# Cached keys and values in rows of four keys per partition, with the order restored on the way, and two more steps ahead of the sample gate product

## The chip, the cores and the metric

The program runs on one core of one Trainium2 chip. A core has five engines that run side by side, each with its own instruction stream: PE (the matrix engine; its weight loads are listed apart as PEld), DVE (vector), ACT (activation functions and copies), POOL (a second elementwise engine) and SP, which here issues the transfers (DMA) between the chip's large memory and the on-chip memories: SBUF, 128 partitions wide, and PSUM, into which PE writes. The metric is device time in microseconds. The kernel before took 1937.82 us, the median of three runs.

## The reference

One inference step of a one-layer streaming encoder, in float32. There are 1024 new frames of one stream (the prompt) and 16 new frames of each of 8 running streams (the samples), whose past is 1024 cached rows each. The layer runs three token mixers on the same normalised input: a stick-breaking attention ("sb"), a state-space scan (SSD) and a forgetting attention ("fox"). Then follow an output projection, cross-attention and a feed-forward block. What the change touches is the attention of the samples over their cached rows, 4 heads of 64 in each of the two groups:

```python
def sb_attend(q, k, v, q_pos, k_pos):
    z = jnp.einsum('bqhd,bkhd->bhqk', q, k).astype(jnp.float32) * (HEAD_DIM ** -0.5)
    valid = k_pos[None, :] < q_pos[:, None]
    log_keep = jnp.where(valid, jax.nn.log_sigmoid(-z), 0.0)
    after = lax.cumsum(log_keep, axis=3, reverse=True) - log_keep
    w = jnp.where(valid, jnp.exp(jax.nn.log_sigmoid(z) + after), 0.0)
    return jnp.einsum('bhqk,bkhd->bqhd', w, v.astype(jnp.float32)).astype(q.dtype)

def fox_attend(q, k, v, fq, fk, q_pos, k_pos):
    s = jnp.einsum('bqhd,bkhd->bhqk', q, k).astype(jnp.float32) * (HEAD_DIM ** -0.5)
    s = s + (jnp.transpose(fq, (0, 2, 1))[..., :, None] - jnp.transpose(fk, (0, 2, 1))[..., None, :])
    valid = k_pos[None, :] <= q_pos[:, None]
    p = jax.nn.softmax(jnp.where(valid, s, -jnp.inf), axis=-1)
    return jnp.einsum('bhqk,bkhd->bqhd', p, v.astype(jnp.float32)).astype(q.dtype)
...
        sb_k = jnp.concatenate([past['sb_k'].astype(sk.dtype), sk], axis=1)
...
        fcum = jnp.cumsum(jnp.concatenate([past['fox_logf'].astype(jnp.float32), logf], axis=1), axis=1)
        fox_o = fox_attend(fq, fox_k, fox_v, fcum[:, past_len:], fcum, qpos, kpos)
```

The weights of sb need a running product over the keys in their order, and those of fox the running sum `fcum` of the gates, also in the order of the keys.

## The kernel before

**Stages.** The input projections come first (to about 100 us of the span in part, and on beside attention). From about 100 to 760 us runs the attention stage: prompt units and sample units of sb and then of fox, in one list that `pipeline` steps through. A unit is `rows` (scores and weights of up to 128 queries) and, one or two units later, `av` (weights transposed, times values). After each step of the pipeline one step of a generator called the fill is taken, or 1.1 steps once the fill has come to the SSD. The fill holds what remains of the input projections (`dense`, three matmuls for each float32 product: L314, L315, L316), the gate sums `fox_sums` between them, and then the SSD. Each `yield` in the fill ends such a step. What is left of the fill after the attention stage is woven into the output projection, which follows, then cross-attention and feed-forward. A planner built into the framework then sets the order of the instructions on each engine: it has a cost for each instruction, takes the order of the code as the first priority, and gives the lines marked `high_priority` more of it. So a step that is written later moves instructions on all engines, and not only its own.

**A sample unit.** Four units p per group, each of two streams b2 of 16 queries and 4 heads. Its 1024 cached keys come in two halves. `load_k` brings half a stream's keys (512 keys x 256 numbers, 512 KB) from `cache_sb_k` or `cache_fox_k` into a buffer "wr" (L850): partition p gets keys p, 128 + p, 256 + p and 384 + p. Eight transposes (L856) turn them, four into each PSUM tile "pst", and ACT copies each tile, 128 x 512, to "kf" (L857), where a column is a key in its order. Four matmuls side by side (`quads`, L844) make the scores "pss". `sb_rows` then takes two sigmoids on ACT (L504, L505), a product scan against the order of the keys on DVE (L507), and a product on POOL (L132). In `av` the weights are transposed in blocks of 128 keys (L887), ACT copies them (L888), and the products with the values (L896) take 128 keys at a time. The values come by L905 into the buffers "vr", again with keys p, 128 + p and so on in partition p. There are 16 loads of each of the four caches, 64 in all, 64 key copies (L857), and 72 weight transposes, 8 of the nine of each unit for cached keys and one for the new ones. The buffers "wr" (two) also take the weights of the projections (L306), and "vr" and "kf" use the buffers "wh" and "wl" of their splits.

**Prompt rows.** A block of 128 queries against up to 512 keys is a product in two matmuls (L547, L548), and a third (L550) adds the mask in the last block. The scores stand in a "pss" bank until L504 and L505 have read it.

**The gate sums.** `fox_sums` makes running sums of the log gates: for the samples a scan on DVE (L687) into a tile of 32 rows, of which L688 writes each row sixteen times to the scratch `fssc`. L690 reads four pieces of it back. L692 and the product L696 make the sample gate tile `fnew`, which the fox units use. Behind the generator's next `yield` stand transposes for the convolution (L756) and the projections z (L769 stores them).

Of the kernel before, what the change touches and what calls it, by code (L numbers as in the profile page):

```python
# [17 lines left out]
P = 128  # L18
# [44 lines left out]
def tile_hybrid_step(ctx: ExitStack, tc: tile.TileContext, a: dict):  # L63
    nc = tc.nc
    ACT, DVE, POOL, PE, SP = nc.scalar, nc.vector, nc.gpsimd, nc.tensor, nc.sync
# [32 lines left out]
    def xc_t(dt=F32):  # L98
        return xcp.tile([P, 1056], dt, tag="xc", name="xc")

    def sg_t(dt=F32):
        return sgp.tile([P, 512], dt, tag="sg", name="sg")
# [7 lines left out]
    def pd():  # L110
        return ps_t(psd, "d")
# [4 lines left out]
    def pT():  # L116
        return ps_t(pst, "t")
# [34 lines left out]
    ident = cst.tile([P, P], F32, name="ident")  # L152
# [143 lines left out]
    def raw_t():  # L296
        return ring.tile([P, 1056], F32, tag="wr", name="wr", bufs=2)
# [301 lines left out]
    def sg2_t(dt=F32):  # L599
        return ptp.tile([P, 256], dt, tag="so", name="so", bufs=4)  # L600
# [45 lines left out]
    def fox_sums():  # L646
        l = log1p_exp_negabs(lf, [P, NBLK, 4])
        DVE.scalar_tensor_tensor(lf.rearrange("p a b -> p (a b)"), lf.rearrange("p a b -> p (a b)"), 0.0,
                                 l.rearrange("p a b -> p (a b)"), ALU.min, ALU.subtract)
        SP.dma_start(out=a["p_fox_logf"][0, 0].rearrange("(k p) h -> p k h", p=P), in_=lf[:, 0:8, :])  # L650
        SP.dma_start(out=a["s_fox_logf"][0].rearrange("b q h -> (b q) h"), in_=lf[:, 8, :])

        fr = xc_t()
        for hf in range(2):
            tp = pd()
            for b in range(4):
                PE.transpose(tp[:4, b * P:(b + 1) * P], lf[:, 4 * hf + b, :], ident)
            ACT.copy(fr[0:4, hf * 512:(hf + 1) * 512], tp[:4])
        DVE.tensor_tensor_scan(fr[0:4, :SEQ], fr[0:4, :SEQ], fr[0:4, :SEQ], 0.0, ALU.add, ALU.bypass)
        SP.dma_start(out=fc_sc, in_=fr[0:4, :SEQ])  # L660
        tp = pd()
        for b in range(8):
            PE.transpose(tp[:, b * 4:(b + 1) * 4], fr[0:4, b * P:(b + 1) * P], ident[:4, :4])
        DVE.tensor_copy(fqc, tp[:, :32].rearrange("p (b h) -> p b h", h=4))
        yield


        pl0 = sg_t()[:, :256]
        SP.dma_start(out=pl0.rearrange("p (u h) -> p u h", h=4),
                     in_=a["cache_fox_logf"][0].rearrange("b k h -> (b k) h").rearrange("(u p) h -> p u h", p=P))  # L670
        pl1 = sg_t()[:, :256]
        DVE.tensor_copy(pl1.rearrange("p (k b h) -> p k b h", k=8, h=4),
                        pl0.rearrange("p (b k h) -> p k b h", k=8, h=4))
        sr = xc_t()[0:32, :PAST + DEC_S]
        for hf in range(2):
            tp = pd()
            for b in range(4):
                PE.transpose(tp[:32, b * P:(b + 1) * P], pl1[:, (4 * hf + b) * 32:(4 * hf + b + 1) * 32], ident)
            ACT.copy(sr[:, hf * 512:(hf + 1) * 512], tp[:32])
        x8 = sg2_t()  # L680
        DVE.tensor_tensor(out=x8[:, :32].rearrange("p (b h) -> p b h", h=4),
                          in0=lf[:, 8, :].unsqueeze(1).to_broadcast([P, 8, 4]),
                          in1=smask.unsqueeze(2).to_broadcast([P, 8, 4]), op=ALU.mult)
        tp = pd()
        PE.matmul(tp[:32, :16], x8[:, :32], fold, start=True, stop=True)
        ACT.copy(sr[:, PAST:], tp[:32, :16])
        DVE.tensor_tensor_scan(sr, sr, sr, 0.0, ALU.add, ALU.bypass)  # L687
        SP.dma_start(out=fs_sc, in_=sr.unsqueeze(1).to_broadcast([32, DEC_S, PAST + DEC_S]))  # L688
        for p in range(4):
            SP.dma_start(out=fqs[:, p:p + 1], in_=fs_sc[8 * p:8 * p + 8, 0, PAST:PAST + DEC_S])  # L690
        y8 = sg2_t()
        DVE.tensor_tensor(out=y8[0:32, :P].rearrange("p (b t) -> p b t", t=DEC_S),  # L692
                          in0=sr[:, PAST:].unsqueeze(1).to_broadcast([32, 8, DEC_S]),
                          in1=bmask32.unsqueeze(2).to_broadcast([32, 8, DEC_S]), op=ALU.mult)
        tp = pd()
        PE.matmul(tp[:, :P], hsel, y8[0:32, :P], start=True, stop=True)  # L696
        DVE.tensor_copy(fnew, tp[:, :P])
        yield
# [112 lines left out]
    def decode_units(m):  # L811
# [15 lines left out]
        def rows(p):  # L827
# [19 lines left out]
            def load_k(hf, b2):  # L847
                raw = raw_t()
                rv = raw[:, :1024].rearrange("p (k c) -> p k c", c=256)
                SP.dma_start(out=rv, in_=ck[2 * p + b2, hf * 512:(hf + 1) * 512, :]  # L850
                             .rearrange("(k p) c -> p k c", p=P))
                kf = ring.tile([P, 1056], F32, tag=("wh", "wl")[b2], name="kf")
                for nb in range(2):
                    tp = pT()
                    for k in range(4):
                        PE.transpose(tp[:, k * P:(k + 1) * P], rv[:, k, nb * P:(nb + 1) * P], ident)  # L856
                    ACT.copy(kf[:, nb * 512:(nb + 1) * 512], tp)  # L857
                return kf

            def emit_past(hf):  # L860
                def emit(ps):
                    kf = [load_k(hf, b2) for b2 in range(2)]
                    quads(ps, lambda b2, nb: kf[b2][:, nb * 512:(nb + 1) * 512])
                return emit
# [13 lines left out]
        def av(p, w, hold):  # L878
# [4 lines left out]
            for k0 in (0, 4, 8):  # L883
                nk = min(4, 9 - k0)
                tp = pT()
                for k in range(nk):
                    PE.transpose(tp[:, k * P:(k + 1) * P], w[:, (k0 + k) * P:(k0 + k + 1) * P], ident)  # L887
                ACT.copy(wn if k0 == 8 else wt[:, k0 * P:(k0 + 4) * P], tp[:, :nk * P])  # L888

            po = pO()  # L890
# [10 lines left out]
            for hf in range(2):  # L901
                raws = []
                for b2 in range(2):
                    raw = ring.tile([P, 1056], F32, tag=("wh", "wl")[b2], name="vr")
                    SP.dma_start(out=raw[:, :1024].rearrange("p (k c) -> p k c", c=256),  # L905
                                 in_=cv[2 * p + b2, hf * 512:(hf + 1) * 512, :]
                                 .rearrange("(k p) c -> p k c", p=P))
                    raws.append(raw)
                for k in range(4):
                    work += quads(wt[:, (4 * hf + k) * P:(4 * hf + k + 1) * P],  # L910
                                  lambda b2, nb, raws=raws, k=k: raws[b2][:, k * 256 + nb * P:k * 256 + (nb + 1) * P],
                                  False, hf == 1 and k == 3)
# [644 lines left out]
    q = []  # L1557
    drain(x_query(0, q))
    for hd in range(1, 4):
        att = both(hd - 1, q)  # L1560
        q = []
# [375 lines left out]
```

## Time and profile before

| what | value |
|---|---|
| median of three runs | 1937.82 us (1937.67 to 1940.25) |
| profiled execution | 1935.64 us, span 1933.8 us |
| mean granted clock of PE | 0.983 |
| PE busy | 1843.4 us, 95% of the span |
| DVE, ACT, POOL busy | 46%, 42%, 32% |
| moved by DMA | 307.52 MB, 159 GB/s on average |
| stage 100 to 760 us: PE, DVE, ACT, POOL busy | 601.44, 328.02, 327.37, 266.72 us |

The profile is of one execution, and its rows are in microseconds of its span. A row of the timeline gives the start, the length, the engine, the line of the code and the operation with the tile that is written, an arrow and the tiles that are read. In brackets stands how long the engine had been idle and which instruction or transfer ended that. A row of a window gives the busy time of PE, PEld, DVE, ACT and POOL in that stretch with the number of instructions, the clock that PE was granted (1.00 is full speed), the busy share of the DMA engines and the rate in GB/s.

### The profile page before, as it was taken

The numbers are of one execution on the slowest core, as the hardware profiler recorded it, in microseconds if no ns is written. First come the engines' busy times: TensorE is split into PE (matmuls) and PEld (weight loads), VectorE is DVE, ScalarE is ACT, GpSimd is POOL, SyncE is SP. The second block draws the span as 40 slices with busy tenths as digits, with TensorE's granted clock in tenths as the row PEclk, the third lists the DMA queues.
The fourth block names the chain that finished last, engine by engine and source line by source line (L and its number), as shares of the span: only waits on it lengthen the run. The fifth ranks groups of instructions, "written<-read, shape, count | busy, mean of one in ns | idle before, by whom it ended". The sixth has DMA issues, their size and how long they took to land.

```text
span 1933.8 us, 32139 instructions
## 1 busy us (share of the span) xinstructions
PE 1843.4 (95%) x12128; PEld 1646.3 (85%) x12128; DVE 898.4 (46%) x1802; ACT 816.6 (42%) x1702; POOL 628.4 (32%) x918
## 2 busy tenths in 40 slices
PE   7989997999898899999999999999999999999997
PEld 5889776898876677889998888999999999888886
DVE  3421324466646783354445378333333333455554
ACT  6431543444656772143333165333333333344443
POOL 6632415263424563211101213554544443000000
PEclk9999997999999989999999999999999999999999
DMA  9455646455487878435559123322233223557572
GB/s 335 139 163 152 205 124 171 131 147 163 139 256 244 259 236 299 153 124 164 164 166 342 59 95 97 95 69 69 72 78 89 71 69 90 193 195 237 176 241 90
DMA packets 328923, 307.52 MB, mean 159 GB/s; under 512 B 88637, under 2 KB 292517, under 8 KB 328769
## 3 DMA queue, kind: packets, MB, share of 16 engines
q1 hardware_dynamic: 328768, 305.48, 51.5%
q8 instruction: 95, 1.56, 0.3%
q14 instruction: 60, 0.48, 0.1%
HBM read 229.31 MB, written 76.11 MB: 158 GB/s over the span
## 4 chain that ended last, share of the span: by engine, by line
PE 79%; DMA 6%; DVE 4%; ACT 2%; POOL 1%; issue 1%; SPq 0%; ACTq 0%; POOLq 0%; DVEq 0%
PE psd L1804 11%; PE psd L314 9%; PE psd L316 9%; PE psd L315 9%; PE pst L1804 8%; PE pss L1804 4%; PE pss L314 3%; PE pss L315 3%; PE pss L316 3%; PE pso L1804 2%; PE pso L580 2%; PE pst L314 1%; PE pst L315 1%; PE pst L316 1%; PE pst L565 1%
## 5 line engine op out<-in xcount | busy, mean ns | idle before, releaser
L132 POOL TENSOR_TENSOR wl<-wr,wh 128x256 fp32r<-128x256 f32 (+1 forms) x180 | 134.2, 778 | 241.2 <-ACT wh L289 208.9
L314 PE MATMUL psd<-act,wh 128*128 128x384 f32 x576 | 198.5, 345 | 5.2 <-DVE sg L441 2.6
L316 PE MATMUL psd<-act,wl 128*128 128x384 f32 x576 | 197.5, 343 | 0.1
L315 PE MATMUL psd<-act,wh 128*128 128x384 f32 x576 | 197.2, 342 | 0.0
L1804 PE MATMUL pst<-bT,tr 128*128 128x256 f32 (+1 forms) x1068 | 155.0, 293 | 0.0
L1804 PEld LDWEIGHTS pst<-bT,tr 128*128 128x128 f32 x1068 | 144.9, 188 | 0.1
L314 PE MATMUL psd<-wh,act 128*128 128x256 f32 (+3 forms) x414 | 134.2, 327 | 3.9 <-DMA act<-osc 1.1
L316 PE MATMUL psd<-wh,act 128*128 128x512 f32 (+3 forms) x424 | 136.9, 324 | 0.0
L315 PE MATMUL psd<-wl,act 128*128 128x256 f32 (+3 forms) x414 | 133.6, 324 | 0.5 <-POOL wl L132 0.5
L1804 PE MATMUL psd<-bT,tr 128*128 128x320 f32 (+1 forms) x912 | 133.2, 295 | 1.0 <-DVE tr L1651 0.5
L251 POOL TENSOR_SCALAR sm<-sm 128x1 f32<-128x1 f32 (+2 forms) x30 | 9.2, 307 | 377.6 <-ACT y L1899 291.8
L1804 PEld LDWEIGHTS psd<-bT,tr 128*128 128x128 f32 x912 | 124.7, 188 | 1.9 <-DVE tr L1651 0.7
L314 PEld LDWEIGHTS psd<-act,wh 128*128 128x128 f32 x576 | 109.3, 190 | 9.3 <-DVE sg L441 3.4
L132 POOL TENSOR_TENSOR tr<-u,tr 128x256 fp32r<-128x256 f32 x110 | 82.9, 782 | 99.2 <-ACT tr L1647 81.7
L132 POOL TENSOR_TENSOR ws<-ws 128x256 f32<-128x256 f32 (+2 forms) x100 | 78.5, 813 | 112.2 <-DVE ws L507 84.5
L316 PEld LDWEIGHTS psd<-act,wl 128*128 128x128 f32 x576 | 109.1, 189 | 2.0 <-issue 1.3
L315 PEld LDWEIGHTS psd<-act,wh 128*128 128x128 f32 x576 | 109.3, 190 | 0.8 <-issue 0.6
L1779 DVE TENSOR_TENSOR tr<-tr,pst 128x256 f32<-128x256 f32 (+1 forms) x86 | 38.6, 449 | 137.5 <-ACT tr L1776 104.4
L132 POOL TENSOR_TENSOR tr<-raw,tr 128x256 fp32r<-128x256 f32 x94 | 69.4, 768 | 86.2 <-ACT tr L1647 77.8
L289 ACT CAST wh<-wr 128x1024 fp32r<-128x1024 f32 (+2 forms) x45 | 47.0, 1050 | 106.2 <-PE psd L316 42.6
L314 PEld LDWEIGHTS psd<-wh,act 128*128 128x128 f32 x414 | 79.5, 192 | 11.9 <-issue 1.7
L1647 ACT CAST tr<-tr 128x384 fp32r<-128x384 f32 (+1 forms) x70 | 37.7, 538 | 122.0 <-DMA tr<-hidsc 112.8
(597 smaller groups left out, 4709.1 us busy)
## 6 DMA issues: line engine op xcount, KB each, us to landing
u<-w_down SPq DMA_DIRECT2D x40, 512.0 KB
raw<-w_down SPq DMA_DIRECT2D x26, 512.0 KB
st<-qksc SPq DMA_DIRECT2D x48, 256.0 KB
wr<-w_in SPq DMA_DIRECT2D x22, 512.0 KB
tr<-hidsc SPq DMA_DIRECT2D x57, 192.0 KB
hidsc<-tr SPq DMA_DIRECT2D x34, 288.0 KB
qksc<-sg SPq DMA_DIRECT2D x48, 192.0 KB
wr<-cache_sb_k SPq DMA_DIRECT2D x16, 512.0 KB
```

The source lines that it names most:

```text
L132: POOL.tensor_tensor(out=out[:, a0:a1], in0=in0[:, a0:a1], in1=in1[:, a0:a1], op=op)
L251: POOL.tensor_scalar(v, ss, inv, EPS, ALU.mult, ALU.add)
L289: ACT.copy(hi[:, :n], raw[:, :n])
L314: PE.matmul(out, ah, bh, start=start, stop=False)
L315: PE.matmul(out, ah, bl, start=False, stop=False)
L316: PE.matmul(out, al, bh, start=False, stop=stop)
L565: PE.transpose(tp[:, o:o + P], w[:, (2 * kp + j) * P:(2 * kp + j + 1) * P], ident)
L580: return PE.matmul(po[r:r + 64, q_], vt[:, 2 * (k0 + i) + j, :], pfs[i][:, sl], start=start and k0 == 0 and (j == 0 or qp > 0), stop=k0 + ...
L1647: ACT.copy(hi, src)
L1779: DVE.tensor_tensor(out=at(out, g), in0=at(x, g), in1=ps[g][:, :GW[g]], op=op)
L1804: PE.matmul(dst[g][:, :GW[g]], x[:, ka], y[:, k, :], start=start and k == 0 and m == 0, stop=stop and k == 3 and m == 2, skip_group_check= ...
```

## The change

The cached keys and values are loaded with four consecutive keys to a partition: partition p of a half gets keys 4p to 4p + 3, which lie side by side in memory, 4 KB in one run, where four runs of 1 KB stood before. Tile k of the four then holds keys k, 4 + k, 8 + k and so on. For the keys, the copy out of PSUM puts the order back: it reads the 512 columns with a step of 128 (k fastest) and writes them side by side. For the values, the weights are brought to the same order: each transpose of cached keys' weights reads every fourth column as its 128. The transposes, copies and products are as many and as large as before. Apart from that, two `yield`s more stand in `fox_sums` between the reads of `fssc` and the product for `fnew`.

```diff
--- before.py
+++ after.py
@@ -688,6 +688,8 @@
         SP.dma_start(out=fs_sc, in_=sr.unsqueeze(1).to_broadcast([32, DEC_S, PAST + DEC_S]))
         for p in range(4):
             SP.dma_start(out=fqs[:, p:p + 1], in_=fs_sc[8 * p:8 * p + 8, 0, PAST:PAST + DEC_S])
+        yield
+        yield
         y8 = sg2_t()
         DVE.tensor_tensor(out=y8[0:32, :P].rearrange("p (b t) -> p b t", t=DEC_S),
                           in0=sr[:, PAST:].unsqueeze(1).to_broadcast([32, 8, DEC_S]),
@@ -847,14 +849,16 @@
             def load_k(hf, b2):
                 raw = raw_t()
                 rv = raw[:, :1024].rearrange("p (k c) -> p k c", c=256)
+
                 SP.dma_start(out=rv, in_=ck[2 * p + b2, hf * 512:(hf + 1) * 512, :]
-                             .rearrange("(k p) c -> p k c", p=P))
+                             .rearrange("(p k) c -> p k c", k=4))
                 kf = ring.tile([P, 1056], F32, tag=("wh", "wl")[b2], name="kf")
                 for nb in range(2):
                     tp = pT()
                     for k in range(4):
                         PE.transpose(tp[:, k * P:(k + 1) * P], rv[:, k, nb * P:(nb + 1) * P], ident)
-                    ACT.copy(kf[:, nb * 512:(nb + 1) * 512], tp)
+                    ACT.copy(kf[:, nb * 512:(nb + 1) * 512].rearrange("c (p k) -> c p k", k=4),
+                             tp.rearrange("c (k p) -> c p k", k=4))
                 return kf
 
             def emit_past(hf):
@@ -884,7 +888,9 @@
                 nk = min(4, 9 - k0)
                 tp = pT()
                 for k in range(nk):
-                    PE.transpose(tp[:, k * P:(k + 1) * P], w[:, (k0 + k) * P:(k0 + k + 1) * P], ident)
+                    wk = w[:, 8 * P:9 * P] if k0 == 8 else \
+                        w[:, k0 * P:(k0 + 4) * P].rearrange("q (p k) -> q p k", k=4)[:, :, k]
+                    PE.transpose(tp[:, k * P:(k + 1) * P], wk, ident)
                 ACT.copy(wn if k0 == 8 else wt[:, k0 * P:(k0 + 4) * P], tp[:, :nk * P])
 
             po = pO()
@@ -904,7 +910,7 @@
                     raw = ring.tile([P, 1056], F32, tag=("wh", "wl")[b2], name="vr")
                     SP.dma_start(out=raw[:, :1024].rearrange("p (k c) -> p k c", c=256),
                                  in_=cv[2 * p + b2, hf * 512:(hf + 1) * 512, :]
-                                 .rearrange("(k p) c -> p k c", p=P))
+                                 .rearrange("(p k) c -> p k c", k=4))
                     raws.append(raw)
                 for k in range(4):
                     work += quads(wt[:, (4 * hf + k) * P:(4 * hf + k + 1) * P],
```

Lines after the two `yield`s are two higher in the changed kernel (L698 for L696, L758 for L756, L771 for L769), and further down three to six higher (L859 for L856, L902 for L896, L911 for L905, L853 for L850). Three places of the changed order follow; all are in the attention stage.

The first place is the sample gate product. On PE, before, it stands behind three prompt rows ("psd<-so,hsel" is the product, "psd<-ident,xc" the transposes behind it):

```order
L547 MATMUL pss<-st 128x128
L548 MATMUL pss<-st 128x128
L550 MATMUL pss<-mask_sb,identr 128x128
L547 MATMUL pss<-st 128x256
L548 MATMUL pss<-st 128x256
L550 MATMUL pss<-mask_sb,identr 128x128
L547 MATMUL pss<-st 128x384
L548 MATMUL pss<-st 128x384
L550 MATMUL pss<-mask_sb,identr 128x128
L696 MATMUL psd<-so,hsel 128x128
L756 MATMUL psd<-ident,xc 128x24 x8
L314 MATMUL psd<-wh,act 128x264
```

After, a piece of 512 keys from a fourth row has come in ahead of it:

```order
L547 MATMUL pss<-st 128x256
L548 MATMUL pss<-st 128x256
L550 MATMUL pss<-mask_sb,identr 128x128
L547 MATMUL pss<-st 128x384
L548 MATMUL pss<-st 128x384
L550 MATMUL pss<-mask_sb,identr 128x128
L547 MATMUL pss<-st 128x512
L548 MATMUL pss<-st 128x512
L550 MATMUL pss<-mask_sb,identr 128x128
L698 MATMUL psd<-so,hsel 128x128
L758 MATMUL psd<-ident,xc 128x24 x8
L314 MATMUL psd<-wh,act 128x264
```

That piece of L547, L548 and L550 stood 48 dense matmuls behind the product before. On POOL, before, the splits of a weight tile (wl) stand ahead of the last piece of a prompt row (ws, 127 wide):

```order
L132 TENSOR_TENSOR ws<-ws 128x256 x3
L132 TENSOR_TENSOR wl<-wr,wh 128x256 x4
L132 TENSOR_TENSOR wl<-wr,wh 128x32
L132 TENSOR_TENSOR ws<-ws 128x127
L834 MEMSET st 128x128
```

After, they stand behind it:

```order
L132 TENSOR_TENSOR ws<-ws 128x256 x3
L132 TENSOR_TENSOR ws<-ws 128x127
L132 TENSOR_TENSOR wl<-wr,wh 128x256 x4
L132 TENSOR_TENSOR wl<-wr,wh 128x32
L836 MEMSET st 128x128
```

The last piece of the row has moved ahead of five pieces of the splits.

The second place is SP at the same time, with the scratch of the gate sums (fssc, fqs) and the value loads of the sample unit. Before:

```order
L688 DMA fssc<-xc 512x1x1040
L850 DMA wr<-cache_sb_k 128x4x256
L596 DMA mixsc<-sg 64x2x256
L690 DMA fqs<-fssc 128x1x1 x4
L769 DMA zsc<-sg 128x256 x3
L905 DMA vr<-cache_sb_v 128x4x256 x2
```

After:

```order
L596 DMA mixsc<-sg 64x2x256
L688 DMA fssc<-xc 512x1x1040
L853 DMA wr<-cache_sb_k 128x1024
L690 DMA fqs<-fssc 128x1x1 x4
L771 DMA zsc<-sg 128x256
L911 DMA vr<-cache_sb_v 128x1024 x2
```

One store of z, not three, stands between the reads of fssc and the pair of value loads now, and the store to mixsc comes first. On PE that sample unit's products with the values (pso<-vr,st), before, stand behind 48 dense matmuls, two row pieces of 512 keys, 48 more dense matmuls and the row's end:

```order
L316 MATMUL psd<-wh,act 128x264
L547 MATMUL pss<-st 128x128
L548 MATMUL pss<-st 128x128
L550 MATMUL pss<-mask_sb,identr 128x128
L896 MATMUL pso<-pt,so 32x128 x4
L896 MATMUL pso<-vr,st 32x128 x16
L314 MATMUL psd<-wh,act 128x264
L315 MATMUL psd<-wl,act 128x264
L316 MATMUL psd<-wh,act 128x264
```

After, the first sixteen stand behind the first 48 dense matmuls and one product of a row:

```order
L315 MATMUL psd<-wl,act 128x264
L316 MATMUL psd<-wh,act 128x264
L547 MATMUL pss<-st 128x512
L902 MATMUL pso<-pt,so 32x128 x4
L902 MATMUL pso<-vr,st 32x128 x16
L314 MATMUL psd<-wh,act 128x264
L315 MATMUL psd<-wl,act 128x264
L316 MATMUL psd<-wh,act 128x264
```

The other sixteen come after 24 more dense matmuls, as before, and now also after the four remaining matmuls of the row.

The third place is a half's fourth key load of a later sample unit, on PE. Before, its transposes (the five of them ahead of "pst<-ident,ws") come right behind the scores of the first half:

```order
L315 MATMUL psd<-act,wh 128x384
L316 MATMUL psd<-act,wl 128x384
L856 MATMUL pst<-ident,wr 128x128 x15
L844 MATMUL pss<-kf,st 32x512 x4
L856 MATMUL pst<-ident,wr 128x128 x5
L565 MATMUL pst<-ident,ws 128x128 x4
L856 MATMUL pst<-ident,wr 128x128 x3
L565 MATMUL pst<-ident,ws 128x128 x7
L314 MATMUL psd<-act,wh 128x384
```

After, eight dense matmuls stand between:

```order
L859 MATMUL pst<-ident,wr 128x128 x8
L846 MATMUL pss<-kf,st 32x512 x4
L314 MATMUL psd<-act,wh 128x384
L315 MATMUL psd<-act,wh 128x384
L316 MATMUL psd<-act,wl 128x384
L314 MATMUL psd<-act,wh 128x384
L315 MATMUL psd<-act,wh 128x384
L316 MATMUL psd<-act,wl 128x384
L314 MATMUL psd<-act,wh 128x384
L315 MATMUL psd<-act,wh 128x384
L859 MATMUL pst<-ident,wr 128x128 x4
```

The transposes of that load now begin with four, eight matmuls later.

## The prediction

> **What bounds the kernel now.** I read the page first, for the engine that is short, and then the busy time by stretches.
>
> ```profile
> span 1933.8 us, 32139 instructions
> PE 1843.4 (95%) x12128; PEld 1646.3 (85%) x12128; DVE 898.4 (46%) x1802; ACT 816.6 (42%) x1702; POOL 628.4 (32%) x918
> ```
>
> The matrix engine PE is busy for 95% of the span; no other engine reaches half, weight loads apart. A part of the change is worth only what it takes from PE's idle time or from the time PE runs at a low granted clock. The stretches (start:end, length, then PE, PEld, DVE, ACT, POOL busy with counts, granted clock, DMA share, GB/s) say where that can be.
>
> ```profile
> 100.00:760.00 660.00, 601.44 (x4433) 518.53 (x4432) 328.02 (x730) 327.37 (x716) 266.72 (x400) 0.96 0.65 194
> 303.50:311.50 8.00, 1.59 (x11) 1.46 (x10) 7.53 (x9) 0.78 (x3) 8.00 (x8) 0.50 0.67 161
> 311.50:317.20 5.70, 5.67 (x26) 5.67 (x27) 1.21 (x2) 1.25 (x3) 5.58 (x13) 0.50 0.98 199
> 321.00:326.80 5.80, 5.80 (x49) 5.76 (x48) 1.89 (x5) 1.90 (x5) 1.23 (x2) 1.00 0.27 79
> 600.00:700.00 100.00, 84.67 (x699) 65.83 (x695) 78.39 (x213) 73.37 (x164) 58.76 (x97) 0.95 0.87 264
> 760.00:800.00 40.00, 40.00 (x177) 32.55 (x176) 9.63 (x14) 5.83 (x6) 11.29 (x16) 1.00 0.45 143
> ```
>
> The attention stage, 100 to 760, holds everything the change touches, and 660.00 − 601.44 = 58.6 us of PE idle. The second and third rows are the sample gate: 8 us with 1.59 busy, and then 5.70 us in which 26 dense matmuls run at clock 0.50, where 5.80 us at 1.00 hold 49. The stall thus costs some 6.3 us of waiting and about 2.8 of slow clock. The last row, the output projection, has no gap. PE's waits from 160 to 760 (total, times, longest) name the parties.
>
> ```profile
> PE psd L696 <- DVE so L692: 6.3, 1, 6.3
> PE pst L856 <- DMA wr<-cache_sb_k: 5.5, 4, 1.8
> PE pst L856 <- DMA wr<-cache_fox_k: 4.7, 4, 1.5
> PE pso L896 <- DMA vr<-cache_sb_v: 3.5, 2, 2.0
> PE pss L844 <- ACT kf L857: 1.2, 1, 1.2
> PE pst L856 <- ACT kf L857: 0.9, 2, 0.7
> ```
>
> The gate product is the longest, 6.3 us. Of 64 cache loads ten are waited for, 5.5 + 4.7 + 3.5 = 13.7 us in all; the other 54 land in time, so their rows are worth nothing. The copies that will be strided cost PE 2.1 us now.
>
> **The loads' rows: −1.5.** Each load moves the same 512 KB, in 4 KB runs instead of four of 1 KB. A cached-key load in the chain of waits, its transposes, and the DMA rate from 203.4 in steps of 0.1 us; then the issue of a feed-forward weight, which has 4 KB runs already, and the rate from 1703.4:
>
> ```profile
> 203.45 3.64 DMA wr<-cache_sb_k
> GB/s 0 0 0 0 0 0 0 0 0 0 0 82 164 174 51 10 123 195 307 379 379 410 369 379 399 379 399 369 384 287 220 230 230 225 174 154 154 143 143 102
> 1703.46 0.33 SPq L1879 DMA_DIRECT2D raw<-w_down  x1
> GB/s 0 0 0 0 0 0 0 0 0 0 328 82 328 205 164 246 410 369 287 492 328 492 410 343 364 364 317 272 415 384 261 215 123 16 0 0 0 0 0 0
> ```
>
> The 1 KB runs already move 370 to 410 GB/s once going, and the 4 KB ones average about the same: no gain per byte. The 4 KB load's data start 0.94 us after its issue against 1.05 and it has no slow tail at the end, though its neighbours differ. I take 0.15 us for each of the ten waits, −1.5. The bounds are 0, and −7 were half of the 13.7 to go.
>
> **The strided reads: 0.** Sixty-four copies out of PSUM and 64 weight transposes change their pattern, not their count or size.
>
> ```profile
> L857 ACT COPY kf<-pst x64: 567/588/655, 184.2 to 722.2; 128x512 f32<-128x512 f32 x64
> L888 ACT COPY st<-pst x8: 587/592/617, 225.2 to 485.0; 128x512 f32<-128x512 f32 x8
> L888 ACT COPY so<-pst x4: 245/268/273, 225.0 to 491.8; 128x128 f32<-128x128 f32 x4
> L887 PEld LDWEIGHTS pst<-ident,ws x72: 137/140/226, 222.1 to 733.7; 128*128 128x128 f32 x72
> L672 DVE COPY sg<-sg 128x256 f32<-128x256 f32 x1 | 0.3, 294 | 4.2 <-DMA sg<-cache_fox_logf 4.2
> 283.29 0.86 PEld L856 LDWEIGHTS pst<-ident,wr 128*128 128x128 f32 x8 [1.68 <-PE pss L844]
> ```
>
> From 128 to 512 elements a copy goes from 268 to 592 ns: (592 − 268)/384 = 0.84 ns an element. The trace has no read with every element apart; the nearest, L672, takes runs of four from strided places and needs 294 ns for 256 elements, as little as plain work, so I take no extra. Were an element twice as dear, a copy would take 588 + 0.84 × 512 = 1018 ns, and 64 of them 27.5 us more on ACT, most of it in ACT's own idle time (327 of 660 us busy). The upper bound is worked out with the rival below: +10. For weights, eight transposes take 0.86 us, 0.11 each, and overlap their loads; doubling 64 loads of 140 ns adds at most 9 us, and 0 if hidden. I take 0 for both; a gain is excluded, as no element is saved.
>
> **The gate product: −0.7.** It waits for DVE's L692, and this depends on POOL and DVE, not on how much PE has to do. Timelines of DVE, POOL and ACT (start, length), then PE:
>
> ```profile
> 302.02 2.66 DVE L507 TENSOR_TENSOR_SCAN ws<-ws 128x1024 f32<-128x1024 f32 x1 [3.29 <-POOL xc L712]
> 304.60 2.68 DVE L687 TENSOR_TENSOR_SCAN xc<-xc 32x1040 f32<-32x1040 f32 x1
> 307.21 1.85 DVE L507 TENSOR_TENSOR_SCAN ws<-ws 128x128 f32<-128x128 f32 x2
> 308.99 0.73 DVE L692 TENSOR_TENSOR so<-xc,bmask 32x128 f32<-32x128 f32 x1
> 307.68 3.70 POOL L132 TENSOR_TENSOR wl<-wr,wh 128x256 fp32r<-128x256 f32 x5
> 311.35 0.41 POOL L132 TENSOR_TENSOR ws<-ws 128x127 f32<-128x127 f32 x1
> 311.79 0.38 ACT L505 ACTIVATE ws<-pss 128x256 f32<-128x256 f32 x1 [1.29 <-POOL ws L132]
> 309.77 0.79 PE L696 MATMUL psd<-so,hsel 32*128 32x128 f32 x2 [6.27 <-DVE so L692]
> 320.00 0.40 PE L547 MATMUL pss<-st 128*128 128x512 f32 x1
> 320.52 0.45 PE L547 MATMUL pss<-st 128*128 128x512 f32 x1
> ```
>
> DVE's four rows run back to back from 302.02 to 309.72 in the old order and in the new one. What the two steps put ahead of the product, by the order shown with the change, is one prompt row of three matmuls: 320.52 − 320.00 = 0.52 us warm, near 1 us at half clock. It needs a score bank that ACT's L505 empties, now at 311.79 and held by POOL's 311.35 row. POOL now takes that row ahead of the 3.70 us of splits, so the bank comes at about 307.7 + 0.41 + 0.38 = 308.5, the row runs from 308.5 to 309.5 inside the wait, and the product still starts near 309.8. Gained: the row's 0.52 us later on and a little clock, −0.7, bounds −1.5 and 0. The rest of the 6.27 stays. Queued behind the product on PE are the 26 slow matmuls above, as before.
>
> **The sample values: +3.** SP's timeline, the landing in the chain of waits, and the two PE rows concerned:
>
> ```profile
> 319.88 2.54 SPq L690 DMA_DIRECT2D fqs<-fssc  x4
> 322.52 3.20 SPq L769 DMA_DIRECT2D zsc<-sg  x3
> 329.06 4.55 DMA vr<-cache_sb_v
> 327.31 1.30 PE pso L896 x40
> 333.66 1.42 PE L896 MATMUL pso<-vr,st 128*32 128x128 f32 x32 [1.97 <-DMA vr<-cache_sb_v]
> ```
>
> SP stands at the reads of fssc until the write of it has landed (319.88; 512 x 1040 elements of 4 bytes, 2.1 MB by the order's row), issues them until 322.42, and only then zsc and the second pair of value loads. In the old order PE gets to the first values at 327.3 and waits 1.97 us for the second pair. In the new one the first values stand behind the first 48 dense matmuls, not behind 96 and two prompt rows. From 311.3: 26 slow matmuls (5.7 us), 22 at 5.80/49 = 0.12 (2.6), one product of a row (0.2), 20 value products (20 × 1.30/40 = 0.65), 24 dense (2.9) and the rest of the row (0.5) bring PE to the second pair at about 324. SP, freed at 322.42, has one zsc (3.20/3 = 1.07) ahead of the pair: issued at 323.5 and 324.0, landed at 324.0 + 4.55 = 328.5. PE waits 4.5, not 1.97: +2.5, and 0.5 for slow clock behind it; +3. Bounds: 0 if the loads land sooner, +5 with 1.7 us (a third of 5) of slow clock after the stall.
>
> **The order of the key waits: −3.** With the steps moved, the planner deals the transposes out otherwise. At 375.06 below PE took up a fourth load right behind the scores of the half before; now eight dense matmuls stand between, at the stage's 601.44/4433 = 0.14 us each some 1.1 us of the 1.70.
>
> ```profile
> 375.06 0.74 PE L856 MATMUL pst<-ident,wr 128*128 128x128 f32 x5 [1.70 <-DMA wr<-cache_sb_k]
> ```
>
> Going through the sixteen places in the new order, I count five or six waits instead of eight, of about the same length: 10.2 × 5.5/8 = 7.0, −3. Bounds −6 and +3: which of these waits survive is the least sure part of the sum.
>
> **The tail: −1.** Two fill steps that stood beside attention (600 to 700: PE 84.7 of 100) end beside the output projection (40.00 of 40.00). Their matmuls leave gaps behind that other work fills only in part; bounds −1.6 and 0.
>
> **Sum.** −1.5 + 0 − 0.7 + 3 − 3 − 1 = −3.2. The profiled execution took 1935.64 us, so 1932.4; the median of the runs, 1937.82, lies 2.18 above it, so **1934.6 us**, with 1929 to 1939 as this forecast's own range. Its runs spread from 1937.67 to 1940.25; less than 0.2%, 3.9 us, can't be told from no change.
>
> **Rivals.**
>
> *The strided reads cost.* Each element of the copy's input lies 512 bytes from the one before, each weight 16 bytes. If ACT pays one more element time per element, a copy takes 1018 ns. For: no row shows such a read at full pace. Against: L672. It decides where PE already waits for copies (1.2 + 0.9 us): a half of the keys needs four copies, and the scores wait for the last. I count six halves as tight, each 4 × 0.43 = 1.7 later: +10, and with the sum's −3.2 + 0.5 for slow clock it is 1937.8 + 7.3 = **1945**. It decides from a copy of about 0.75 us on.
> The Trainium skill, "SBUF — State Buffer", section "Door 1: The DMA port swizzle (why `[64,N]` ≈ `[32,N]`)", speaks against the change here: lines of 16 bytes need two hits each, PSUM's lines are 8 bytes, and "any non-contiguous PSUM access pattern significantly slows down matmuls". It gives no price for a copy, and no run so far shows one.
>
> *The loads land before they are waited for.* If larger rows shorten a load by a microsecond, 0.7 of the 13.7 us of waits go (−9.6), with −0.7 and −1 as above and +1.5 left of the values: 1937.8 − 9.8 = **1928**. For: the longest waits are 1.8, 1.5 and 2.0 us, so that one microsecond would end most of them. Against: the equal GB/s.
>
> *The gate wait goes.* If the moved steps fill it, 6.3 us and 2.8 of slow clock fall away: 1937.8 − 9.1 = **1928.7**. Against: only one row is put there, and DVE's 302.02 to 309.72 is unmoved.
>
> **How the numbers follow.** Forecast 0.52, strided reads 0.25, loads 0.17, gate 0.06. Faster, the same and slower (by 0.2%): from the forecast 0.19, 0.29, 0.04; strided reads 0, 0.04, 0.21; loads 0.14, 0.03, 0; gate 0.05, 0.01, 0. Together 0.38, 0.37, 0.25. The range takes in both other sides, 1926 to 1946.
>
> **What would show it.** Copies at 0.57 to 0.66 us and weight loads at 0.14 confirm the zero, copies near 1.0 the first rival. The gate product should still wait for DVE, 5 us or more, and start at 309 to 311. The second pair of the sample's first values should be waited for 4 to 6 us. The eight waits of key transposes should total 6 to 8 us; under 3 speaks for the loads. I am wrong if PE's idle time from 100 to 760 changes by more than 6 us either way.

## The result and the profile after

The changed kernel took 1925.93 us, the median of six runs (1918.90 to 1928.80), beside 1940.38 us of the kernel before (1937.67 to 1941.10) on the same chip: a ratio of 0.9924 with a 95% interval of 0.9905 to 0.9943. Two later sets of runs gave 0.9937 (0.9912 to 0.9962) and 0.9934 (0.9915 to 0.9954). It is faster by some 0.6 to 0.8%, 11 to 15 us between the medians. The forecast was 1934.6 us and no clear difference; the range ended at 1926, just above the result.

The profiled execution took 1928.8 us, the slowest of its six, and that of the kernel before, 1935.64, was faster than all six of its runs. The two profiles thus show 7 us of the 14.5. The page of the changed kernel:

```profile
span 1926.9 us, 32135 instructions
PE 1842.8 (96%) x12128; PEld 1644.7 (85%) x12128; DVE 899.4 (47%) x1802; ACT 816.7 (42%) x1702; POOL 627.6 (33%) x918
q1 hardware_dynamic: 304192, 305.48, 51.1%
```

PE has the same work, 1842.8 against 1843.4 us; what fell is the time between. The row of the queue counts packets: 24,576 fewer than in the row of the kernel before, for the same 305.48 MB.

```profile
q1 hardware_dynamic: 328768, 305.48, 51.5%
```

To see where time went I took three stretches of the attention stage, and for each the loss: the time in which PE is idle, and the length times what is missing from the clock (which is rounded to a hundredth, so that the product is good to 1.3 us in 260). Idle time at a low clock enters both terms. Before, then after (columns as in the prediction):

```profile
295.00:345.00 50.00, 39.72 (x320) 36.40 (x321) 18.89 (x28) 16.81 (x39) 28.16 (x42) 0.80 0.66 164
345.00:500.00 155.00, 149.55 (x1073) 133.99 (x1071) 93.13 (x158) 77.63 (x169) 69.09 (x93) 1.00 0.52 147
500.00:760.00 260.00, 233.42 (x1762) 185.66 (x1762) 165.29 (x461) 157.58 (x345) 110.54 (x180) 0.94 0.80 250
```

```profile
295.00:345.00 50.00, 38.17 (x287) 33.52 (x287) 20.08 (x26) 17.94 (x40) 31.61 (x42) 0.76 0.63 160
345.00:500.00 155.00, 148.00 (x1058) 131.99 (x1055) 91.11 (x146) 75.07 (x165) 61.99 (x88) 0.99 0.50 145
500.00:760.00 260.00, 240.79 (x1850) 192.25 (x1849) 171.42 (x478) 160.15 (x351) 115.09 (x185) 0.99 0.80 257
```

At the sample gate (295 to 345) the loss went from 10.3 + 0.20 × 50 = 20.3 us to 11.8 + 0.24 × 50 = 23.8, so this place got worse. From 345 to 500 it rose from 5.5 to some 8.6. From 500 on it fell from 26.6 + 0.06 × 260 = 42.2 to 19.2 + 0.01 × 260 = 21.8, by 20 us, of which 7.4 are idle time and 13 are the clock. Where the missing clock is counted in the trace only while PE is busy, the gate goes from 17 to 22 us and the stretch from 500 on from 41 to 23, so the reading stands. Two more profiles of the changed kernel give 22.9 and 21.9 at the gate, 23.7 and 22.8 from 500 on. In the profiles all the gain lies where the fox units run beside the SSD, 180 us and more behind the added steps. Of PE's waits from 160 to 760, those at the gate, for cache loads and for key copies, after:

```profile
PE pss L547 <- ACT ws L505: 4.6, 1, 4.6
PE pso L902 <- DMA vr<-cache_sb_v: 3.8, 1, 3.8
PE pst L859 <- DMA wr<-cache_sb_k: 2.9, 3, 1.5
PE pst L859 <- DMA wr<-cache_fox_k: 2.2, 1, 2.2
PE pss L846 <- ACT kf L860: 1.2, 1, 1.2
PE pst L859 <- ACT kf L860: 1.0, 2, 0.8
```

The waits for cache loads fell from 13.7 us to 2.9 + 2.2 + 3.8 = 8.9, and the strided copies are waited for as long as the plain ones were (1.2 and 1.0). The 6.3 us of the gate product have only moved, to the row piece ahead of it:

```profile
306.74 0.22 PE L550 MATMUL pss<-mask_sb,identr 128*128 128x128 f32 x1
311.57 0.79 PE L547 MATMUL pss<-st 128*128 128x512 f32 x1 [4.60 <-ACT ws L505]
313.17 0.79 PE L698 MATMUL psd<-so,hsel 32*128 32x128 f32 x2 [0.27 <-DVE so L694]
```

### The profile page after: what moved, and what is told of

Its sections match the earlier page's. It is cut to its first block, busy times and chain, and to the rows that moved or that the text cites. A ratio compares the mean times of both kernels' runs of the same rounds, so it can differ in the third digit from the quotient of the medians.

```text
span 1926.9 us, 32135 instructions
## 1 busy us (share of the span) xinstructions
PE 1842.8 (96%) x12128; PEld 1644.7 (85%) x12128; DVE 899.4 (47%) x1802; ACT 816.7 (42%) x1702; POOL 627.6 (33%) x918
## 3 DMA queue, kind: packets, MB, share of 16 engines
q1 hardware_dynamic: 304192, 305.48, 51.1%
## 4 chain that ended last, share of the span: by engine, by line
PE 72%; issue 6%; DMA 6%; DVE 5%; ACT 3%; POOL 2%; SPq 0%; ACTq 0%; POOLq 0%; DVEq 0%
PE psd L1810 11%; PE pst L1810 8%; PE psd L314 8%; PE psd L315 8%; PE psd L316 8%; PE pss L1810 4%; PE pss L314 2%; PE pss L315 2%; PE pss L316 2%; PE pso L1810 2%; DMA act<-acsc 1%; PE pso L580 1%; POOL wl L132 1%; PE pst L314 1%; PE pst L316 1%
## 5 line engine op out<-in xcount | busy, mean ns | idle before, releaser
L132 POOL TENSOR_TENSOR wl<-wr,wh 128x256 fp32r<-128x256 f32 (+1 forms) x180 | 138.2, 800 | 224.7 <-ACT wh L289 188.1
L1810 PE MATMUL psd<-bT,tr 128*128 128x256 f32 (+1 forms) x912 | 132.6, 295 | 0.5 <-DVE tr L1657 0.5
L314 PEld LDWEIGHTS psd<-act,wh 128*128 128x128 f32 x576 | 109.4, 190 | 13.7 <-DVE so L735 5.0
L132 POOL TENSOR_TENSOR ws<-ws 128x256 f32<-128x256 f32 (+2 forms) x100 | 72.8, 756 | 138.2 <-DVE ws L507 113.9
L314 PEld LDWEIGHTS psd<-wh,act 128*128 128x128 f32 x414 | 79.6, 193 | 10.2 <-issue 1.3
```

The source lines that it names most:

```text
L132: POOL.tensor_tensor(out=out[:, a0:a1], in0=in0[:, a0:a1], in1=in1[:, a0:a1], op=op)
L314: PE.matmul(out, ah, bh, start=start, stop=False)
L1810: PE.matmul(dst[g][:, :GW[g]], x[:, ka], y[:, k, :], start=start and k == 0 and m == 0, stop=stop and k == 3 and m == 2, skip_group_check= ...
```

## The experiments

Two theories stood against each other, that the 4 KB rows made the gain, and that the order did in which the planner dealt the work out anew. They can be told apart: where only the pattern of a load is changed, the order of the instructions on every engine stays row for row the same.

**The rows, in four orders.** The first pair puts 1 KB rows into the changed kernel, at both loads:

```diff
-                             .rearrange("(p k) c -> p k c", k=4))
+                             .rearrange("(k p) c -> p k c", p=P))
```

> The changed kernel with the 64 cache loads put back to four runs of 1 KB a partition; strided copies, strided weights and both steps stay, and the order of the instructions on every engine is the changed kernel's own, row for row. (What it leaves out: keys and values are then in another order than the weights, so the attention of the samples is not the reference's.) If the 4 KB rows made the gain (theory of rows): the time goes back up, by 8 to 14 us against the changed kernel, to 1934 to 1940. If the new order made it (theory of order): 1925 to 1929, within 3 us of the changed kernel. By the sum of the prediction, rows were worth 1.5 us.

The second puts 4 KB rows into the kernel before, by the opposite edit.

> The kernel before with nothing changed but the 64 cache loads, now one run of 4 KB a partition; order of all instructions as before, row for row. (The order of keys is not restored, so the attention of the samples is not the reference's.) Theory of rows: 1926 to 1932, most of the gain, and waits of the key transposes and values for DMA falling from 13.7 us to under 5. Theory of order: 1937 to 1940, no difference beyond 0.2%, waits for DMA above 10 us.

The third pair is the layout without the added steps (e3) and the same with 1 KB rows (e9). Against the changed kernel, e3 is this:

```diff
-        yield
-        yield
         y8 = sg2_t()
```

> The changed loads, copies and transposes without the two added steps. Theory of rows: 1926 to 1932. Theory of order, with the gain from the two steps: 1936 to 1940. The strided copies should stay at 0.59 us and strided weight loads at 0.21 us in either case.

> The layout's copies and weights strided, but the loads as before, in 1 KB runs, and no added steps; the order of all instructions is that of the layout alone (1932.4), row for row. (The order of the keys is then wrong, so the attention of the samples is not the reference's.) Third pair for the rows: in the old order they gave -6.1 us, in the changed kernel's -2.3. If the gain of rows is steady at 2 to 6 us: 1934 to 1939. If strided reads cost: above 1940, with the loads' gain then larger.

The fourth is the added steps alone (e5) and the same with 4 KB rows, without strided reads (e10). Against the changed kernel, e10 is:

```diff
-                    ACT.copy(kf[:, nb * 512:(nb + 1) * 512].rearrange("c (p k) -> c p k", k=4),
-                             tp.rearrange("c (k p) -> c p k", k=4))
+                    ACT.copy(kf[:, nb * 512:(nb + 1) * 512], tp)
...
-                        w[:, k0 * P:(k0 + 4) * P].rearrange("q (p k) -> q p k", k=4)[:, :, k]
+                        w[:, (k0 + k) * P:(k0 + k + 1) * P]
```

> The kernel before with the two added steps and nothing else: loads of 1 KB runs, plain copies and weights. If the steps' new order makes most of what is left after the rows (rows alone gave -6.1 us of -12.6), this runs 1929 to 1934. If the order of the changed kernel was lucky because layout and steps were planned together, 1936 to 1941. The gate product waits for DVE or for a score bank, 5 us or more, in either case.

> The changed kernel with plain copies and plain weights: 4 KB loads and two steps, order of the steps alone (1933.6). (The order of the keys is then wrong, so the attention of the samples is not the reference's.) Fourth pair for the rows: 1928 to 1932 if they give 2 to 6 us in this order too; 1933 to 1935 if nothing.

The changed kernel ran again beside the first three.

> The changed kernel once more, beside the others on the same chip: 1919 to 1929 us with a median near 1926, for a second profile of it. In its profile the stage from 500 to 760 us should again hold some 15 to 19 us less idle time and slow clock than before, if that is where the gain lies; the sample gate and the values behind it should again be no better than before.

Medians, and ratios to the kernel before in the same set of runs:

| order of | with 1 KB rows | with 4 KB rows | rows |
|---|---|---|---|
| the kernel before | 1 | 1933.65: 0.9968 (0.9952 to 0.9983) | −0.32% |
| the layout alone | 1939.38: 0.9989 (0.9969 to 1.0009) | 1932.41: 0.9971 (0.9953 to 0.9989) | −0.18% |
| the steps alone | 1933.62: 0.9975 (0.9958 to 0.9992) | 1930.48: 0.9959 (0.9940 to 0.9977) | −0.16% |
| the changed kernel | 1929.39: 0.9943 (0.9927 to 0.9959) | 1927.14: 0.9937 (0.9912 to 0.9962) | −0.06% |

The rows gain in all four, on average (0.32 + 0.18 + 0.16 + 0.06)/4 = 0.18%, 3.5 us. Only the first pair is clear of its interval by itself; taken as independent, the four intervals give 0.05 to 0.31% for the average. Neither theory holds alone: with 1 KB rows the changed order still saves 0.57%, and without steps the rows and strided reads save 0.29%. Of the order's 0.57%, the steps alone give 0.25%, clear of their interval, and the layout's order alone 0.11%, not clear of it; the layout has an order of its own even without steps, on PE from 222 us on. So the strided reads are not isolated by any pair: 0.9971 with them and 0.9968 without are two orders. Neither order with them is slower than its counterpart without, beyond the intervals.

PE's waits for cache loads, in the four orders, went from 13.7 to 11.9 us with 4 KB rows, from 10.8 to 8.3, from 10.9 to 11.6 and from 12.3 to 8.9. In the kernel before they stayed far above the 5 us that the theory of rows expected, although its median fell by 6 us; where the rest of that gain arises the profiles don't show. What a 4 KB row saves in the queue can be read from the page. In the order before and in the changed one, the row of the queue, 4 KB and 1 KB (e2, then e1; the other two are above):

```profile
q1 hardware_dynamic: 304192, 305.48, 51.0%
```

```profile
q1 hardware_dynamic: 328768, 305.48, 51.8%
```

Before: 0.515 × 1933.8 = 995.9 us on each of 16 engines with 1 KB rows, 0.510 × 1934.5 = 986.6 with 4 KB; changed order: 0.518 × 1929.3 = 999.4 and 0.511 × 1926.9 = 984.6. The other two pairs differ by 13 and 9 us. So 9 to 15 us of each engine for 24,576 packets, (9.3 to 14.8) × 16/24,576 = 6 to 10 ns for each packet saved.

Where the order gains shows in the losses of the same eight kernels (1 KB rows, then 4 KB), each from one profile:

| order of | 295 to 345, us | 500 to 760, us |
|---|---|---|
| the kernel before | 20.3, 20.5 | 42.2, 41.7 |
| the layout alone | 18.1, 16.2 | 40.3, 34.4 |
| the steps alone | 24.4, 21.7 | 29.2, 30.3 |
| the changed kernel | 26.5, 23.8 | 26.6, 21.8 |

With the steps the gate is worse and the stretch from 500 on better, in either layout and with either row. The steps alone:

```profile
295.00:345.00 50.00, 37.63 (x288) 32.85 (x288) 20.05 (x26) 18.23 (x40) 30.71 (x42) 0.76 0.74 169
500.00:760.00 260.00, 238.58 (x1823) 190.28 (x1822) 169.91 (x476) 160.46 (x351) 115.35 (x187) 0.97 0.81 254
```

**The steps.** If the two steps had to stand ahead of the product, or if each step gave a fixed gain, these would show it. First both behind the product:

```diff
-        yield
-        yield
         y8 = sg2_t()
...
         DVE.tensor_copy(fnew, tp[:, :P])
         yield
+        yield
+        yield
```

> The changed kernel with the two added steps behind the gate product and not ahead of it. If what counts is that everything after them in the fill comes two steps later (theory of the shift): 1924 to 1931, as the changed kernel. If what counts is that they stand ahead of the product (theory of the gate): 1931 to 1937, as the layout alone.

It took 1927.58 us, 0.9946 (0.9925 to 0.9967): as the changed kernel. The place in the code does not matter here, but the run does not part the two theories: on PE its first 4,547 matmuls, to 705 us, are the changed kernel's, the gate product among them. The planner gave the product the same place on PE. From 500 on its one profile has a loss of 23.4 + 7.8 = 31.2 us all the same, 7.5 to 9.4 above the changed kernel's three; whether by the order of the other engines or by chance stays open. Then other numbers of steps, one, three and four, where the changed kernel has two:

> The changed kernel with one added step, not two. Theory of the shift as a steady trend (each step that leaves the attention stage saves about 2.5 us): 1929 to 1931, between the layout alone (1932.4) and the changed kernel (1927.1). If the order falls as it happens to fall: anything from 1924 to 1938.

> The changed kernel with three added steps. In its order the 32 products with the sample's values stand ahead of the gate product, so the gate's wait should shrink from some 4.6 to 3 us or less and the wait for values near 331 go, some 8 to 10 us with the slow clock. If the time follows the gate: 1917 to 1922. If each dealing falls as it happens to fall, as with one step (1935.1): anything from 1924 to 1946, with the gate's gain given back in other stretches.

> The changed kernel with four added steps; its order at the gate has one piece of 512 keys of a later row ahead of the product. A steady gain per step would give 1920 to 1925; a dealing by chance 1924 to 1946. With 0, 1, 2 and 3 steps it shows whether the number of steps has a trend.

| steps added | 0 | 1 | 2 | 3 | 4 |
|---|---|---|---|---|---|
| median, us | 1932.41 | 1935.12 | 1927.14 | 1926.24 | 1942.00 |
| ratio | 0.9971 | 0.9987 | 0.9937 | 0.9933 | 1.0011 |
| interval | 0.9953 to 0.9989 | 0.9971 to 1.0003 | 0.9912 to 0.9962 | 0.9910 to 0.9955 | 0.9995 to 1.0027 |

There is no trend, and with four steps nothing of the gain is left. That two steps deal the work well is luck, as far as these runs tell. Three steps do what a reader of the profile would want at the gate, and this gate is much better than the changed kernel's, yet the time is the same. Its two stretches:

```profile
295.00:345.00 50.00, 44.82 (x376) 40.37 (x374) 18.30 (x35) 19.11 (x47) 22.79 (x36) 0.90 0.64 146
500.00:760.00 260.00, 235.19 (x1774) 185.22 (x1774) 163.82 (x452) 150.76 (x332) 106.46 (x175) 0.97 0.79 251
```

The gate's loss is 5.2 + 5.0 = 10.2 us, 13.6 less than in the changed kernel; from 500 on it is 24.8 + 7.8 = 32.6, 10.8 more. In the profiles, the gain at one place was given back at the other. Another attempt at the gate moved the four reads of fssc behind the product, with two steps more behind it:

```diff
-        for p in range(4):
-            SP.dma_start(out=fqs[:, p:p + 1], in_=fs_sc[8 * p:8 * p + 8, 0, PAST:PAST + DEC_S])
...
         DVE.tensor_copy(fnew, tp[:, :P])
         yield
+        yield
+        yield
+        for p in range(4):
+            SP.dma_start(out=fqs[:, p:p + 1], in_=fs_sc[8 * p:8 * p + 8, 0, PAST:PAST + DEC_S])
```

> The changed kernel, with the four reads of fssc moved behind the gate product and two more steps, so that SP does not stand at them ahead of the value loads. In its order all four value loads of the sample unit come ahead of the write of fssc, and its 36 products with the values stand ahead of the gate product. The values' wait of 3.8 us near 331 should go and the wait ahead of the product shrink from some 4.6 to 2 to 3; if nothing else moves, 1920 to 1924. If the new dealing elsewhere takes it back, 1925 to 1932.

The waits did go as expected. Two of some length are left from 295 to 345, the gate's and one for which the profile shows no releaser:

```profile
PE pso L580 <- issue: 2.7, 1, 2.7
PE psd L696 <- DVE so L692: 2.6, 1, 2.6
```

But the median was 1945.98 us, 1.0030 (1.0017 to 1.0043), slower than the kernel before. Its profile (1936.5 us) is of the fastest of its twelve runs and does not show the loss in full.

**The two places apart.** If the gain lies from 500 us on, it must be possible to have it with another gate. The first kernel (three less one) takes three steps ahead of the product and one out further on, so that from the second z projection on its order is nearly the changed kernel's, behind the gate of three steps. Against the changed kernel:

```diff
         yield
         yield
+        yield
         y8 = sg2_t()
...
                 dt_softplus()
-                yield
```

> Three added steps ahead of the gate product, and one taken out behind it (the yield after dt_softplus), with the new layout. At the gate the order is that of three steps (values ahead of the product), and from the second projection z on nearly that of the changed kernel. If the gain of the changed kernel lies in how work is dealt from 500 us on, and the gate's loss adds to it: gate stretch 295 to 345 with under 8 us idle, stretch 500 to 760 with 19 to 21 us idle, and 1916 to 1922 us. If gains at one place are given back at the next in any dealing: 1925 to 1930.

The second (steps behind dt) leaves the gate as in the layout alone and puts the two steps behind it:

```diff
-        yield
-        yield
         y8 = sg2_t()
...
                 dt_softplus()
                 yield
+                yield
+                yield
```

> The new layout with no step added in fox_sums, and two added behind dt_softplus instead: the gate has the order of the layout alone, the stage from 500 us on nearly that of the changed kernel. If the steps' gain lies from 500 us on: 1924 to 1929, as the changed kernel or a little better, and 17 to 21 us idle from 500 to 760. If it lies at the gate: 1931 to 1934, as the layout alone (1932.4).

> The changed kernel beside the two others on the same chip: 1925 to 1929.

| kernel | median, us | ratio |
|---|---|---|
| three less one | 1919.74 | 0.9905 (0.9872 to 0.9938) |
| steps behind dt | 1921.77 | 0.9916 (0.9892 to 0.9939) |
| changed kernel | 1927.15 | 0.9934 (0.9915 to 0.9954) |

Stretches of the layout alone, of the steps behind dt, and of three less one:

```profile
295.00:345.00 50.00, 42.33 (x348) 38.12 (x345) 18.56 (x31) 16.72 (x41) 27.48 (x40) 0.83 0.65 171
500.00:760.00 260.00, 233.43 (x1781) 182.96 (x1780) 162.95 (x455) 156.19 (x340) 108.79 (x180) 0.97 0.79 255
```

```profile
295.00:345.00 50.00, 39.21 (x340) 35.10 (x338) 20.33 (x30) 18.51 (x42) 30.57 (x42) 0.90 0.70 177
500.00:760.00 260.00, 239.82 (x1827) 189.69 (x1826) 170.43 (x478) 160.16 (x349) 111.69 (x181) 0.99 0.79 253
```

```profile
295.00:345.00 50.00, 44.08 (x357) 39.20 (x357) 18.15 (x33) 19.05 (x44) 25.90 (x39) 0.86 0.69 161
500.00:760.00 260.00, 238.27 (x1799) 189.42 (x1798) 166.81 (x471) 157.04 (x345) 111.40 (x181) 0.97 0.78 251
```

Losses at the gate and from 500 on: layout alone 16.2 and 34.4, steps behind dt 15.8 and 22.8, three less one 12.9 and 29.5. The second kernel has the gate's loss of the layout alone and from 500 on the changed kernel's, and is clear of the layout alone (0.9971, 0.9953 to 0.9989). So the steps' gain needs nothing at the gate; it goes with the later order. The steps behind dt came out below their expected 1924 to 1929 us; three less one came into its range of time, but with 21.7 us idle from 500 on, where 19 to 21 were expected. Against the changed kernel both have lower medians, by 5 and 7 us, though the intervals overlap. The best time of this study is theirs.

## Why the prediction was wrong

**The missing term.** The step that failed is the one on order: it went through the places where PE waits for a cache load or at the gate, and priced the new order there and in the tail, −0.7 + 3 − 3 − 1 = −1.7 us together. The new order with 1 KB rows, the strided reads in it, measured −0.57%, 11 us. The shift moves the order of everything behind it, and the waits that went are mostly not for loads; the clock behind these had no term at all. PE's five longest waits from 500 to 760, before and in the changed kernel:

```profile
PE pss L547 <- DVE sm L521: 5.4, 3, 3.9
PE pst L856 <- DMA wr<-cache_fox_k: 4.7, 4, 1.5
PE pso L896 <- DVE sm L254: 3.1, 1, 3.1
PE psd L1017 <- DMA act<-xbcsc: 2.9, 3, 1.0
PE pss L314 <- ACT wh L289: 1.8, 1, 1.8
```

```profile
PE pss L547 <- DVE sm L521: 3.7, 8, 1.1
PE psd L1101 <- ACT sg L1099: 3.4, 1, 3.4
PE psd L1069 <- DVE sg L438: 3.0, 2, 2.0
PE pst L859 <- DMA wr<-cache_fox_k: 2.2, 1, 2.2
PE psd L1023 <- DMA act<-xbcsc: 0.9, 1, 0.9
```

A stall of 3.9 us on the maxima of the fox rows (L521) became eight of at most 1.1; that on L254 went, that on the scratch of xbc shrank, and 3.4 on L1099 came. With 1 KB rows in the same order (e1) the stretch was:

```profile
500.00:760.00 260.00, 241.21 (x1835) 193.45 (x1834) 169.32 (x476) 160.46 (x351) 113.93 (x184) 0.97 0.82 256
```

Its loss is 18.8 + 7.8 = 26.6 us, against 42.2 before and 21.8 in the changed kernel, so most of the fall is order: 7.8 us idle and 7.8 of clock. That these waits are the reason is read from the profile; no run took one of them away alone. The stage as a whole, after:

```profile
100.00:760.00 660.00, 607.55 (x4464) 522.02 (x4463) 330.53 (x732) 327.16 (x716) 265.19 (x400) 0.97 0.64 196
```

Idle time fell from 58.6 to 52.5 us, 6.1, just past the 6 us that the prediction named as its sign of being wrong; the two other profiles of the changed kernel show falls of 4.2 and 5.1. A sign in idle time alone misses the clock, where more of the loss from 500 on went.

**The rows, −1.5.** The size was low: −1.2 to −6.2 us by the four pairs, 3.5 on average, inside the bounds of −7 and 0. The waits for cache loads changed by −1.8, −2.5, +0.7 and −3.4 us, on average about the −1.5 predicted for them; the rest was not in the sum. The step "no gain per byte", read from the GB/s of one 4 us window with other transfers in it, could not see 6 to 10 ns a packet; the queue's time on the page does. The Trainium skill, "DMA: Bandwidth & Descriptors", section "Why small descriptors are slow (HBM only)", gives a fixed overhead of about three cycles for each packet; the direction agrees with the 6 to 10 ns here.

**The strided reads, 0: right, as far as shown.** The copies and the weight loads after:

```profile
L860 ACT COPY kf<-pst x64: 562/588/629, 185.3 to 712.5; 128x512 f32<-128x512 f32 x64
L893 PEld LDWEIGHTS pst<-ident,ws x72: 138/209/230, 223.4 to 732.9; 128*128 128x128 f32 x72
```

A copy reads PSUM with a step of 512 bytes as fast as without one, 588 ns. A weight load with a step of 16 bytes does cost, 209 instead of 140 ns, 64 × 69 = 4.4 us in all. Most of it is hidden: in the traces, transposes one behind another start 120 ns apart instead of 109 at full clock, 64 × 11 = 0.7 us of PE's time, and PE's waits show none of it. The rule of the Trainium skill, "SBUF — State Buffer", section "Door 1: The DMA port swizzle (why `[64,N]` ≈ `[32,N]`)", that a new line for every read costs, agrees with the weights here (+69 ns). What it says of PSUM is about matmuls, and the copies show nothing of the kind.

**The gate, −0.7.** The stall stayed, 6.3 us before and 4.6 + 0.3 on two instructions after, but not where it was predicted: the product was to wait 5 us or more for DVE and start by 311, and it started at 313.17 behind a row that waited for ACT. That row was expected to run within the wait, at 308.5; it began at 311.57, since the score bank came with ACT's L505 at 311.13, which waited for POOL. POOL's row, its last piece, DVE beside it, and ACT:

```profile
304.90 6.19 POOL L132 TENSOR_TENSOR ws<-ws 128x256 f32<-128x256 f32 x4
308.68 2.42 POOL L132 TENSOR_TENSOR ws<-ws 128x127 f32<-128x127 f32 x1
308.20 2.68 DVE L687 TENSOR_TENSOR_SCAN xc<-xc 32x1040 f32<-32x1040 f32 x1
311.13 0.38 ACT L505 ACTIVATE ws<-pss 128x256 f32<-128x256 f32 x1 [4.16 <-POOL ws L132]
```

The last piece of POOL's row comes ahead of the splits, as the order said, but it ran beside DVE's scan of 1040 elements and took 2.42 us, not the 0.41 that it took behind the scan before and that the sum used. The whole place ran 3.4 us later, and more of it at low clock (0.76 against 0.80). In the two other profiles of the changed kernel the product started at 308.42 and 313.10, and the row ahead waited 5.5 and 4.6 us.

**The sample values, +3; the key waits, −3; the tail, −1.** The second pair was waited for 3.8 us, against 4.5 expected and 1.97 before: +1.8. The key waits fell from 10.2 to 5.1 us and from eight to four: −5.1, in the bounds of −6 and +3, more than the five or six counted. In the stretch of the output projection PE was busy without a gap as before.

**The rivals.** Strided reads on the slower side fell with the 588 ns. "The loads land before they are waited for" gave 1928, nearest to the result in time but not for its reason: rows alone make 1933.65. "The gate wait goes" is refuted for this kernel; with three steps it shrinks to 1.2 us, and the time does not follow.

## What to carry to other kernels

Where a planner sets the order, a step added in one place is a change to all that follows, and its price cannot be read at the place of the edit. Before crediting such a change, run the edit's parts in one and the same order, and the shift of the order without the edit; try other shifts too, since a good one may be luck. A stall that is repaired is worth only what the later stretches do not give back, so compare the loss, idle time and missing clock, stretch by stretch.

## What was not expected of the hardware

Reading PSUM with a step of 512 bytes costs ACT nothing in a copy of 128 x 512 (588 ns either way), while reading SBUF with a step of 16 bytes makes the load of 128 columns of weights half as long again (140 to 209 ns). Runs of 4 KB instead of 1 KB save 6 to 10 ns of queue time for each packet less, although both showed some 370 to 410 GB/s in the short rows that the prediction read. A product of 128 x 127 on POOL took 2.42 us beside a long scan on DVE, and 0.41 without one.
